# A one-layer hybrid decoder block on one core: the first 512 columns loaded slice by slice from one array, and attention issued for two pairs of heads at a time

## The chip, the core and the metric

One core of a Trainium2 chip runs one program. The metric is the device time of one execution in microseconds (us); lower is better. Engines are named as in the profile: PE (TensorE; PEld is its weight load, which runs beside its matmuls), DVE (VectorE), ACT (ScalarE), POOL (GpSimd), SP (SyncE, here only an issuer of DMAs).

## The reference, cut to what matters

256 tokens, width 1024, one layer. The normed input is multiplied with one wide matrix, whose columns feed four token mixers: a state-space scan (A), three softmax attentions (B block attention with a bias table, C with a forget-gate bias, D a sliding window with sinks; 8 heads of 64 each), and four gates.

```python
proj = h @ w_in
(m_z, m_xbc, m_dt, b_qkv, c_qkv, c_f, d_q, d_kv, gate_logits) = jnp.split(proj, SPLIT_POINTS, axis=-1)
y_a = mamba2_branch(m_z, m_xbc, m_dt, conv_w, conv_b, dt_bias, a_log, d_skip, ssm_norm_w)
y_b = moba_attention(heads(bq, N_HEADS), heads(bk, N_HEADS), heads(bv, N_HEADS), rel_bias[:, :N_HEADS])
...
# each branch is projected, scaled by its sigmoid gate and summed; w_out; residual; RMSNorm; SwiGLU; residual; RMSNorm
```

Everything is float32. A product keeps that precision by splitting each operand in two parts, "hi" (rounded) and "lo" (what is left), and adding three matmuls: hi·hi, hi·lo, lo·hi.

## The kernel before, in words

**Weights** come as a stream of pieces of about 1 MB, in the order of `FIRST` and `stream()`: `xbc0`, `xbc1`, `n0`, `qkB0`, `vB0`, ... then gates `g...`, branch projections `wb...`, `wo`, `gu` and `dn`. SP fetches a piece into one of three `raw` buffers; ACT makes its `hi` copy, DVE its `lo`. For each piece PE runs groups of matmuls: 48 matmuls of 256 columns for a piece, or 24 of 512 columns.

**The start.** `xbc0` and `xbc1` are two pieces of 256 columns. `xT` (the input, transposed) comes in six DMAs, `xbc0` in six more beside them, the channel constants `chan` in one. For each chunk ACT makes `xx` (x scaled, hi) and `hi_xbc`, DVE the lo parts, and PE follows (L440). PE has run 8 matmuls on ones before (`warm`). `xbc1` is then a piece of its own (L250 to L253), after it `n0`, whose matmuls write the tiles `n`.

**The weaver.** The order on every engine is written when the program is built. `Weaver` keeps rough clocks of PE, DVE and ACT; after each group of matmuls (`wv.tick`) it lets waiting tasks issue their next step, if their buffers are free and their DVE and ACT work ends within a slack of PE's clock. The tasks are generators; each `yield Need(...)` is a step.

**Attention** is one task for a pair of heads, `att_pair` (12 of them). Steps: a DMA of bias rows; four score matmuls into tiles `s` (L764, L766; each head uses 64 of PE's 128 rows); DVE adds the bias and takes the minimum of the negated scores (L777, L779), for C after two more operations (L849, L851); ACT takes the exponential (`p`); DVE scales `p`; PE transposes it (`pt`); ACT copies that to SBUF (`pts`); four matmuls of probabilities with values into `y` (`pv`, L685 and L687; each head uses 64 of PE's columns); ACT and DVE split `y`. The scan has one block of the same shape as `pv` for each of four pairs (`ya`). Between these blocks PE runs matmuls of the full 128 rows and columns; in the PEld rows the form stands as 128*128, 64*128 (scores) or 128*64 (`pv`). PSUM tiles of tasks come from the pool `att` (5 buffers), those of the groups from `acc` (3).

Of the kernel before, what the change touches and what calls it, by code (L numbers as in the profile page):

```python
# [199 lines left out]
def hybrid_block_kernel(ctx: ExitStack, tc: tile.TileContext, A, out):  # L200
# [225 lines left out]
    px = [att("xbc0_%d" % j, [128, 256]) for j in range(2)]  # L426
    parts["xbc0"] = h0, l0 = [wp.tile([128, WMAX], F32R, tag=n, name=n + "_xbc0", bufs=3) for n in ("hi", "lo")]
    hb, lb, wb = (cut(t, 8, 256) for t in (h0, l0, w0))
    for a, b in chunks:
        for k in range(a, b):  # L430
            act.activation(xx(k)[:, 0, :], xT[k // 4][:, k % 4, :], AF.Copy, scale=nm_mix[:, k : k + 1])
        act.activation(hb[:, a:b, :], wb[:, a:b, :], AF.Copy)
        for k in range(a, b):
            dve.scalar_tensor_tensor(xx(k)[:, 1, :], xT[k // 4][:, k % 4, :], nm_mix[:, k : k + 1],
                                     xx(k)[:, 0, :].bitcast(F32), ALU.mult, ALU.subtract)
        dve.tensor_tensor(lb[:, a:b, :], wb[:, a:b, :], hb[:, a:b, :].bitcast(F32), ALU.subtract)
        for w, i in ((hb, 0), (hb, 1), (lb, 0)):
            for k in range(a, b):
                for j in range(2):
                    pe.matmul(px[j], w[:, k, tok(j)], xx(k)[:, i, :], start=k == 0 and w is hb and i == 0,  # L440
                              stop=k == 7 and w is lb)
    wv.later(lambda: end_of("xbc0", px), [])
# [310 lines left out]
    def att_pair(br, j, heads, load_rows, q, k, vs, addend, sinks=None):  # L753
        yield Need(rows=1)
        rw = load_rows()
        yield Need()
# [13 lines left out]
        for i in range(2):  # L770
            nm_ = "%s%d" % (br, heads[i])
            s = ss[i]
            a0, a1 = addend(rw, i)
            neg = work("sp" + nm_, [128, 384], "sp")
            nm = work("nm" + nm_, [128, 2], "nm")
            init = BIG if sinks is None else sinks[:, heads[i] : heads[i] + 1]
            dve.tensor_tensor_reduce(out=neg[:, 128:384], in0=s[:, 128:384], in1=a1, scale=-1.0, scalar=init,  # L777
                                     op0=ALU.add, op1=ALU.min, accum_out=nm[:, 1:2])
            dve.tensor_tensor_reduce(out=neg[:, 0:128], in0=s[:, 0:128], in1=a0, scale=-1.0, scalar=init,  # L779
                                     op0=ALU.add, op1=ALU.min, accum_out=nm[:, 0:1])  # L780
            p = work("p" + nm_, [128, 384], "pp")
            sm = work("sm" + nm_, [128, 2], "sm")
# [11 lines left out]
        for i in range(2):  # L794
            p, sm = pp[i], sms[i]
            if sinks is not None:
                dve.tensor_tensor(sm, sm, exs[i], ALU.add)
                rel(rs=1)
# [527 lines left out]
```

## Time and profile before

| | |
|---|---|
| median of 3 runs | 521.33 us (520.48 to 521.71) |
| profiled execution, its own time | 519.55 us |
| its span, first to last instruction | 517.8 us |
| PE busy | 507.6 us, 98% of the span, 3106 matmuls |
| PE weight loads | 444.1 us |
| DVE / ACT / POOL busy | 350.6 / 284.1 / 29.7 us |
| DMA | 96.06 MB, 186 GB/s over the span |

PE is busy nearly all the time, but the matmuls are pipelined and a busy PE is not one at its peak. What can shorten the kernel is seen in the start times of PEld rows: how far apart two weight loads of the same kind stand when something lies between them.

### The profile page before, as it was taken

The numbers are of one execution on the slowest core, as the hardware profiler recorded it, in microseconds if no ns is written. First come the engines' busy times: TensorE is split into PE (matmuls) and PEld (weight loads), VectorE is DVE, ScalarE is ACT, GpSimd is POOL, SyncE is SP. The second block draws the span as 40 slices with busy tenths as digits, with TensorE's granted clock in tenths as the row PEclk, the third lists the DMA queues.
The fourth block names the chain that finished last, engine by engine and source line by source line (L and its number), as shares of the span: only waits on it lengthen the run. The fifth ranks groups of instructions, "written<-read, shape, count | busy, mean of one in ns | idle before, by whom it ended". The sixth has DMA issues, their size and how long they took to land.

```text
span 517.8 us, 7989 instructions
## 1 busy us (share of the span) xinstructions
PE 507.6 (98%) x3106; PEld 444.1 (86%) x3106; DVE 350.6 (68%) x658; ACT 284.1 (55%) x511; POOL 29.7 (6%) x61
## 2 busy tenths in 40 slices
PE   7999999999999999999999999999999999999995
PEld 6998998987897778888888899998888888888884
DVE  4577778898896947547386494688676676673435
ACT  6667464567575863443444363876655655543412
POOL 2008110012110000000000000000000000000001
PEclk8999999999999999999999999999999999999998
DMA  7974464465355244727537283355545555585302
GB/s 230 388 277 173 162 217 150 156 217 192 137 177 183 82 164 162 250 92 280 191 128 278 89 332 148 97 229 177 219 173 172 215 184 169 210 313 181 144 0 82
DMA packets 17122, 96.06 MB, mean 186 GB/s; under 512 B 2235, under 2 KB 3563, under 8 KB 6844
## 3 DMA queue, kind: packets, MB, share of 16 engines
q1 hardware_dynamic: 15660, 91.15, 48.8%
q0 software_dynamic: 1424, 4.41, 3.1%
q8 instruction: 24, 0.39, 0.3%
q14 instruction: 14, 0.11, 0.1%
HBM read 94.46 MB, written 1.09 MB: 185 GB/s over the span
## 4 chain that ended last, share of the span: by engine, by line
PE 95%; issue 2%; DMA 1%; ACT 1%; DVE 1%; SPq 0%; POOL 0%; POOLq 0%; ACTq 0%; DVEq 0%
PE pg L989 17%; PE gu L260 13%; PE pd L1186 11%; PE pb L250 8%; PE gu L262 7%; PE pvC L989 2%; PE pvB L989 2%; PE qkC L252 2%; PE po L250 1%; PE gu L250 1%; PE gu L253 1%; PE po L253 1%; PE gu L252 1%; PE qkC L250 1%; PE po L252 1%
## 5 line engine op out<-in xcount | busy, mean ns | idle before, releaser
L260 PE MATMUL gu<-x3x,hi_gu 128*128 128x512 f32 x288 | 72.1, 392 | 0.0
L989 PE MATMUL pg<-hi_g,xx 128*128 128x512 f32 x256 | 64.3, 393 | 0.0
L260 PEld LDWEIGHTS gu<-x3x,hi_gu 128*128 128x128 f32 x288 | 51.8, 189 | 9.3
L989 PEld LDWEIGHTS pg<-hi_g,xx 128*128 128x128 f32 x256 | 47.4, 188 | 11.1 <-issue 1.5
L339 DVE TENSOR_TENSOR lo_gu<-raw_gu,hi_gu 128x1024 fp32r<-128x1024 f32 x44 | 53.2, 1216 | 1.4 <-ACT hi_gu L331 1.4
L331 ACT ACTIVATE hi_g<-raw_g 128x1024 fp32r<-128x1024 f32 x32 | 32.9, 1053 | 29.0 <-DMA raw_g<-in_w_dram 14.2
L331 ACT ACTIVATE hi_gu<-raw_gu 128x1024 fp32r<-128x1024 f32 x44 | 45.6, 1051 | 1.5 <-PE gu L253 1.5
L1186 PE MATMUL pd<-hi_dn,aa 128*128 128x512 f32 (+1 forms) x176 | 46.2, 384 | 0.0
L339 DVE TENSOR_TENSOR lo_g<-raw_g,hi_g 128x1024 fp32r<-128x1024 f32 x32 | 38.1, 1219 | 8.8 <-ACT hi_g L331 8.8
L262 PEld LDWEIGHTS gu<-x3x,lo_gu 128*128 128x128 f32 x288 | 39.3, 190 | 2.8
L339 DVE TENSOR_TENSOR lo_dn<-raw_dn,hi_dn 128x1024 fp32r<-128x1024 f32 x22 | 26.1, 1220 | 21.6 <-ACT hi_dn L331 21.5
L262 PE MATMUL gu<-x3x,lo_gu 128*128 128x256 f32 x288 | 40.2, 282 | 0.0
L1186 PEld LDWEIGHTS pd<-hi_dn,aa 128*128 128x128 f32 x176 | 32.6, 188 | 6.5
L331 ACT ACTIVATE hi_dn<-raw_dn 128x1024 fp32r<-128x1024 f32 x22 | 22.4, 1052 | 25.3 <-PE pd L1186 25.3
L1128 DVE TENSOR_TENSOR gs<-gu,ge 128x256 f32<-128x256 f32 x36 | 15.3, 424 | 30.7 <-ACT ge L1127 30.6
L989 PE MATMUL pg<-lo_g,xx 128*128 128x512 f32 x128 | 34.3, 389 | 0.0
L1127 ACT ACTIVATE ge<-gu 128x256 f32<-128x256 f32 x36 | 13.5, 374 | 27.5 <-PE gu L262 27.3
L989 PEld LDWEIGHTS pg<-lo_g,xx 128*128 128x128 f32 x128 | 24.0, 188 | 5.1
L1186 PE MATMUL pd<-lo_dn,aa 128*128 128x512 f32 (+1 forms) x88 | 26.7, 384 | 0.0
L339 DVE TENSOR_TENSOR lo_wb<-raw_wb,hi_wb 128x1024 fp32r<-128x1024 f32 x16 | 19.3, 1220 | 9.3 <-ACT hi_wb L331 9.3
L913 ACT ACTIVATE gate<-pg,r1h 128x512 f32<-128x512 f32 x16 | 11.0, 687 | 25.7 <-PE pg L989 25.7
L929 DVE SCALAR_TENSOR_TENSOR gp<-gate,pb 128x512 f32<-128x512 f32 x12 | 8.2, 687 | 21.2 <-PE pb L250 20.9
(326 smaller groups left out, 1140.5 us busy)
## 6 DMA issues: line engine op xcount, KB each, us to landing
raw_gu<-in_w_dram SPq DMA_DIRECT2D x22, 1024.0 KB, 4.8
...
```

Source lines behind the costliest of these rows:

```text
L250: pe.matmul(o, l, r, start=start, stop=stop)
L252: pe.matmul(o, l, r[:, 0, :], start=start, stop=False)
L253: pe.matmul(o, l, r[:, 1, :], start=False, stop=stop)
L260: pe.matmul(o, wh(k), x(k), start=start and i == 0, stop=False)
L262: pe.matmul(o[:, 0, :], wl(k), x(k)[:, 0, :], start=False, stop=stop and i == n - 1)
L331: act.activation(parts[name][0][:, s], raws[name][:, s], AF.Copy)
L339: dve.tensor_tensor(lo[:, s], raws[name][:, s], hi[:, s].bitcast(F32), ALU.subtract)
L913: act.activation(gates[b, t][:, 512 * nh : 512 * nh + 512], p, AF.Tanh, scale=r1h[:, t : t + 1])
L989: pe.matmul(pg[t], l, r, start=kh == 0 and i == 0, stop=kh == 1 and i == len(terms) - 1)
L1127: act.activation(e[:, j, :], p[j][:, 1, :], AF.Copy)
L1128: dve.tensor_tensor(s[:, j, :], p[j][:, 0, :], e[:, j, :], ALU.add)
L1186: pe.matmul(o, l, r, start=start and j == 0, stop=stop and j == len(terms) - 1)
```

## The change

Two parts. First, `xbc0` and `xbc1` become one piece of 512 columns. Its weights are put beside `xT` in one DRAM array, `head`, after the channel constants: 64 columns of constants, and then for each of the 8 slices of the inner dimension 256 columns of `xT` and 512 of weights. SP loads it in 9 DMAs into tiles `hd0` to `hd7`; POOL's queue loads no part of it. For each slice PE runs 12 matmuls: 4 blocks of output columns, three products each. The four accumulators are two `att` and two `acc` tiles. The next pieces' DMAs (`n0`, x in natural order, `qkB0`, and now `vB0`) follow on SP.

Second, `att_quad` takes the place of `att_pair`: one task runs two pairs. The scores of both pairs are one step (8 matmuls), the transposes stay one step for each pair, and the `pv` matmuls of both pairs are one step (8 matmuls). There are 6 such tasks. A quad takes its `p`, `sm` and `pts` buffers ahead (`hold`) and needs four `att` tiles at once.

```diff
-FIRST = ("xbc0 xbc1 n0 qkB0 vB0 vB1 xbc2 qkB1 xbc3 z0 qkB2 z1 qkB3 qD0 qkC0 vC0 vC1 qkC1 qD1 qkC2 qkC3").split()
+FIRST = ("xbc0 n0 qkB0 vB0 vB1 xbc2 qkB1 xbc3 z0 qkB2 z1 qkB3 qD0 qkC0 vC0 vC1 qkC1 qD1 qkC2 qkC3").split()
...
-    cols["xbc0"], cols["xbc1"] = rng(BM0, 256), rng(CM0, 256)
+    cols["xbc0"] = rng(BM0, 512)
...
-    chunks = ((0, 1), (1, 2), (2, 4), (4, 6), (6, 7), (7, 8))
-    for a, b in chunks:
-        nc.sync.dma_start(xT[a // 4][:, a % 4 : (b - 1) % 4 + 1, :], A["xT"][:, a:b, :])
-        src = bass.AP(tensor=A["w"].tensor, offset=woff["xbc0"] + 256 * a, ap=[[2048, 128], [1, 256 * (b - a)]])
-        (nc.sync if a else pool).dma_start(w0[:, 256 * a : 256 * b], src)
-        if a == 0:
-            nc.sync.dma_start(chan, A["chan"])
-    fetch(names[1], 4)
-    fetch(names[2])
+    hd = [slot("hd%d" % i, (128, 832 if i == 0 else 768)) for i in range(8)]
+    at_ = 0
+    for i in range(8):
+        for n in (320, 512) if i == 0 else (768,):
+            o_ = 320 if n == 512 else 0
+            nc.sync.dma_start(hd[i][:, o_ : o_ + n], A["head"][:, at_ : at_ + n])
+            at_ += n
+    fetch(names[1])
...
+    px = [(att, acc)[j // 2]("xbc0_%d" % j, [128, 256]) for j in range(4)]
+    for k in range(8):
+        xk, wk_ = hd[k][:, -768:-512], hd[k][:, -512:]
+        hb, lb = (t[:, k % 4, :] for t in hl[k // 4])
+        s = hd[0][:, k : k + 1]
+        act.activation(xx(k)[:, 0, :], xk, AF.Copy, scale=s)
+        act.activation(hb, wk_, AF.Copy)
+        dve.scalar_tensor_tensor(xx(k)[:, 1, :], xk, s, xx(k)[:, 0, :].bitcast(F32), ALU.mult, ALU.subtract)
+        dve.tensor_tensor(lb, wk_, hb.bitcast(F32), ALU.subtract)
         for w, i in ((hb, 0), (hb, 1), (lb, 0)):
+            for j in range(4):
+                pe.matmul(px[j], w[:, tok(j)], xx(k)[:, i, :], start=k == 0 and w is hb and i == 0,
+                          stop=k == 7 and w is lb)
+    pool.tensor_copy(chan, hd[0][:, 0:64])
...
-    def att_pair(br, j, heads, load_rows, q, k, vs, addend, sinks=None):
+    def att_quad(br, pairs, addend, sinks=None):
...
+        yield Need(pe=1360, att=4, pp=4, sm=4)
+        hold(pp=4, sm=4)
...
+        for ss, (_, _, _, q, k, _) in zip(sss, pairs):
+            for i in range(2):
+                pe.matmul(ss[i][:, 0:128], q[hs[i], 0:128], k[hs[i], 0:128], start=True, stop=True)
+        for ss, (_, _, _, q, k, _) in zip(sss, pairs):
+            for i in range(2):
+                pe.matmul(ss[i][:, 128:384], q[hs[i], 128:256], k[hs[i], 0:256], start=True, stop=True)
...
+        yield Need(pe=1300, att=2)
+        ys = [att("y%s%d" % (br, p[0]), [128, 256]) for p in pairs]
+        for y, sts, p in zip(ys, stss, pairs):
+            pv(y, p[5], sts)
...
-    for j in range(4):
-        wv.later(lambda j=j: moba_pair(j), ["qkB%d" % j, "vB0", "vB1", "erow"], True)
+    for js in ((0, 1), (2, 3)):
+        wv.later(lambda js=js: moba_quad(js), ["qkB%d" % j for j in js] + ["vB0", "vB1", "erow"], True)
```

**SP's queue, the first rows of the program, before.** The names are tiles and DRAM arrays; sizes are partitions x float32.

```order
L395 DMA xT0_81<-in_xT_dram 128x256
L399 DMA chan_79<-in_chan_dram 128x64
L395 DMA xT0_81<-in_xT_dram 128x256
L397 DMA raw_xbc0_83<-in_w_dram 128x256
L395 DMA xT0_81<-in_xT_dram 128x512
L397 DMA raw_xbc0_83<-in_w_dram 128x512
L395 DMA xT1_82<-in_xT_dram 128x512
L397 DMA raw_xbc0_83<-in_w_dram 128x512
L395 DMA xT1_82<-in_xT_dram 128x256
L397 DMA raw_xbc0_83<-in_w_dram 128x256
L395 DMA xT1_82<-in_xT_dram 128x256
L397 DMA raw_xbc0_83<-in_w_dram 128x256
```

After these stand `xbc1` in four DMAs of 128x512 and then `n0`. The same place of the changed program:

```order
L400 DMA hd0_80<-in_head_dram 128x320
L400 DMA hd0_80<-in_head_dram 128x512
L400 DMA hd1_81<-in_head_dram 128x768
L400 DMA hd2_82<-in_head_dram 128x768
L400 DMA hd3_83<-in_head_dram 128x768
L400 DMA hd4_84<-in_head_dram 128x768
L400 DMA hd5_85<-in_head_dram 128x768
L400 DMA hd6_86<-in_head_dram 128x768
L400 DMA hd7_87<-in_head_dram 128x768
L328 DMA raw_n0_98<-in_w_dram 128x2176
L412 DMA xn0_100<-in_x_dram 128x1024
```

The bytes ahead of `n0` are the same; they are now in 9 DMAs of up to 393 KB where 17 stood (one of them POOL's), with rows of 3 KB instead of 1 or 2 KB, and each slice's `xT` and weights arrive together.

**PE after the piece `xbc3`, before**: the `y` of the first pair of B, and then the scores of its second pair (`sB2`, `sB3`), between the last matmul of `xbc3` and the first of `z0`. The scores of the first pair stand alone, 92 rows earlier.

```order
L250 MATMUL xbc3_763<-xx3_119,lo_xbc3_609 128x256 x2
L685 MATMUL yB0_850<-ptsB0_846,vB_565 64x256
L685 MATMUL yB0_850<-ptsB1_848,vB_565 64x256
L687 MATMUL yB0_850<-ptsB0_846,vB_565 64x128
L687 MATMUL yB0_850<-ptsB1_848,vB_565 64x128
L764 MATMUL sB2_858<-qkB0_438 128x128
L764 MATMUL sB3_859<-qkB0_438 128x128
L766 MATMUL sB2_858<-qkB0_438 128x256
L766 MATMUL sB3_859<-qkB0_438 128x256
L252 MATMUL z0_864<-xx0_116,hi_z0_697 128x256
```

The same place of the changed program, where the scores of both pairs stand together:

```order
L255 MATMUL xbc3_731<-xx3_117,lo_xbc3_610 128x256 x2
L774 MATMUL sB0_806<-qkB0_444 128x128
L774 MATMUL sB1_807<-qkB0_444 128x128
L774 MATMUL sB2_808<-qkB0_444 128x128
L774 MATMUL sB3_809<-qkB0_444 128x128
L777 MATMUL sB0_806<-qkB0_444 128x256
L777 MATMUL sB1_807<-qkB0_444 128x256
L777 MATMUL sB2_808<-qkB0_444 128x256
L777 MATMUL sB3_809<-qkB0_444 128x256
L257 MATMUL z0_818<-xx0_114,hi_z0_683 128x256
```

Their `y` blocks have moved to the middle of the piece `qD0`, four pieces later, also together:

```order
L255 MATMUL qD0_1179<-xx3_117,lo_qD0_1039 128x256 x2
L689 MATMUL yB0_1209<-ptsB0_1041,vB_568 64x256
L689 MATMUL yB0_1209<-ptsB1_1043,vB_568 64x256
L691 MATMUL yB0_1209<-ptsB0_1041,vB_568 64x128
L691 MATMUL yB0_1209<-ptsB1_1043,vB_568 64x128
L689 MATMUL yB1_1210<-ptsB2_1175,vB_568 64x256
L689 MATMUL yB1_1210<-ptsB3_1177,vB_568 64x256
L691 MATMUL yB1_1210<-ptsB2_1175,vB_568 64x128
L691 MATMUL yB1_1210<-ptsB3_1177,vB_568 64x128
L257 MATMUL qD0_1179<-xx0_114,hi_qD0_1038 128x256
```

Over the whole program the places where PE leaves full 128*128 matmuls for scores or `pv` go from 21 to 16. Before they are: scores alone 7 times, one `y` (or `ya`) alone 8 times, `y` and then scores 4 times, two `y` and then scores once, two `y` once. After: scores of a quad 6 times, `y` of a quad 6 times, `ya` alone 4 times. The attentions also end later: the last `y` of C stood before the first `wb` piece, and now stands in the last gate piece; D's last `y` stands before the piece that uses it, by 36 matmuls of 512 columns.

## Rows read from the trace of the kernel before

**Rows 1.** Waits of PE and of PEld: engine, line, who was waited for; us in total, times, longest.

```profile
PE xbc L440 <- ACT hi_xbc L432: 2.3, 2, 2.1
...
PE yB L685 <- ACT ptsB L815: 0.9, 1, 0.9
```

**Rows 2.** Stretches of the start: us, then busy time (instructions) of PE, PEld, DVE, ACT, POOL, the granted clock, DMA share, GB/s.

```profile
2.00:5.00 3.00, 2.86 (x14) 2.56 (x13) 0.25 (x1) 1.00 (x5) 1.74 (x5) 1.00 0.88 230
5.00:9.00 4.00, 2.08 (x12) 1.88 (x12) 1.98 (x6) 1.95 (x6) 0.00 (x0) 1.00 0.91 268
9.00:14.00 5.00, 4.74 (x27) 4.74 (x28) 4.86 (x11) 4.21 (x10) 0.00 (x0) 0.66 0.98 297
14.00:21.00 7.00, 7.00 (x61) 7.00 (x60) 3.11 (x5) 3.85 (x5) 0.00 (x0) 1.00 1.00 414
```

**Rows 3.** The start in order of time, PE, PEld and ACT: start us, us, engine, line, operation, tiles, shape, count, idle time before and who ended it.

```profile
1.08 3.78 PE L424 MATMUL warm<-cumu 128*128 128x128 f32 x16 [1.08 <-DVE cumu L383]
5.08 1.12 PE L440 MATMUL xbc<-xx,hi_xbc 128*128 128x256 f32 x4 [0.22 <-ACT hi_xbc L432]
6.28 0.64 PE L440 MATMUL xbc<-xx,hi_xbc 128*128 128x256 f32 x4
6.76 0.40 PE L440 MATMUL xbc<-xx,lo_xbc 128*128 128x256 f32 x2
9.26 2.01 PE L440 MATMUL xbc<-xx,hi_xbc 128*128 128x256 f32 x8 [2.10 <-ACT hi_xbc L432]
15.06 0.19 PEld L252 LDWEIGHTS xbc<-xx,hi_xbc 128*128 128x128 f32 x1
20.82 2.06 PEld L250 LDWEIGHTS n<-hi_n,xx 128*128 128x128 f32 x16
...
4.21 0.51 ACT L431 ACTIVATE xx<-xT,chan 128x256 fp32r<-128x256 f32 x1 [1.99 <-DMA chan<-in_chan_dram]
18.41 2.12 ACT L331 ACTIVATE hi_n<-raw_n 128x1088 fp32r<-128x1088 f32 x2 [2.15 <-DMA raw_n<-in_w_dram]
```

**Rows 4.** Groups of ACT instructions of one shape: count, busy us, mean ns of one, idle time before and who ended it.

```profile
L431 ACT ACTIVATE xx<-xT,chan 128x256 fp32r<-128x256 f32 x8 | 3.8, 500 | 4.3 <-DMA xT<-in_xT_dram 2.3 <-DMA chan<-in_chan_dram 2.0
L432 ACT ACTIVATE hi_xbc<-raw_xbc 128x512 fp32r<-128x512 f32 x2 | 1.2, 614 | 0.0
```

**Rows 5.** PEld in order of time: groups of 12 matmuls of 512 columns (`pg`, 8 hi and 4 lo) with nothing between them; here the first rows of the first and of the seventh.

```profile
268.55 1.77 PEld L989 LDWEIGHTS pg<-hi_g,xx 128*128 128x128 f32 x8
...
284.87 0.19 PEld L989 LDWEIGHTS pg<-hi_g,xx 128*128 128x128 f32 x1
```

**Rows 6.** PEld in order of time, blocks of attention between such groups.

```profile
158.79 1.68 PEld L989 LDWEIGHTS pg<-hi_g,xx 128*128 128x128 f32 x8
...
163.41 1.68 PEld L989 LDWEIGHTS pg<-hi_g,xx 128*128 128x128 f32 x8 [0.33 <-issue]
...
166.35 0.30 PEld L764 LDWEIGHTS sD<-kD,qD 64*128 64x128 f32 x4 [0.35 <-issue]
166.57 0.31 PEld L766 LDWEIGHTS sD<-kD,qD 64*128 64x128 f32 x4
167.21 0.76 PEld L989 LDWEIGHTS pg<-hi_g,xx 128*128 128x128 f32 x4 [0.33 <-issue]
...
180.57 1.68 PEld L989 LDWEIGHTS pg<-hi_g,xx 128*128 128x128 f32 x8
...
183.50 0.20 PEld L685 LDWEIGHTS yD<-ptsD,vD 128*64 128x64 f32 x4 [0.35 <-issue]
...
184.31 1.70 PEld L989 LDWEIGHTS pg<-hi_g,xx 128*128 128x128 f32 x8 [0.17 <-issue]
```

**Rows 7.** PEld in order of time: two `y` and then scores between two groups of `pvC` (12 matmuls of 512 columns), and two `y` alone between halves of `qkC` (24 matmuls of 256 columns).

```profile
112.70 1.77 PEld L989 LDWEIGHTS pvC<-hi_vC,xx 128*128 128x128 f32 x8
...
118.05 1.69 PEld L989 LDWEIGHTS pvC<-hi_vC,xx 128*128 128x128 f32 x8 [0.33 <-issue]
...
146.27 0.19 PEld L252 LDWEIGHTS qkC<-xx,hi_qkC 128*128 128x128 f32 x1
...
150.79 0.19 PEld L252 LDWEIGHTS qkC<-xx,hi_qkC 128*128 128x128 f32 x1 [0.17 <-issue]
```

**Rows 8.** Stretches, columns as in rows 2: the attention part, and the parts in which gates and branch projections run.

```profile
58.00:130.00 72.00, 71.10 (x548) 64.02 (x548) 62.61 (x147) 44.22 (x88) 7.70 (x11) 1.00 0.55 186
130.00:192.00 62.00, 62.00 (x435) 50.50 (x435) 48.89 (x160) 41.05 (x114) 3.86 (x6) 1.00 0.44 151
192.00:203.60 11.60, 11.60 (x57) 9.42 (x54) 5.80 (x7) 5.38 (x7) 0.00 (x0) 1.00 0.26 91
203.60:225.40 21.80, 21.80 (x98) 18.06 (x97) 11.27 (x10) 9.23 (x11) 0.00 (x0) 1.00 0.67 242
```

**Rows 9.** DVE groups of C's softmax, columns as in rows 4.

```profile
L851 DVE SCALAR_TENSOR_TENSOR f<-cr,cumn,amask 128x256 f32<-128x256 f32 x8 | 3.8, 477 | 0.0
L777 DVE CUSTOM_DVE_ANT_0 spC<-sC,f 128x256 f32<-128x256 f32 x8 | 3.4, 424 | 1.5 <-PE qkC L253 0.5
L849 DVE SCALAR_TENSOR_TENSOR f<-cr,cumn,amask 128x128 f32<-128x128 f32 x8 | 2.8, 345 | 0.0
L779 DVE CUSTOM_DVE_ANT_0 spC<-sC,f 128x128 f32<-128x128 f32 x8 | 2.3, 285 | 0.0
L777 DVE DVE_READ_ACCUMULATOR2_ANT nmC<- 128x1 f32 x8 | 0.7, 82 | 0.0
```

More of the change, by code (lines that the diff above doesn't have):

```diff
@@ L228, in rel, with hold @@
             wv.free[t] += n
+    def hold(**tags):
+        for t, n in tags.items():
+            wv.free[t] -= n
     def acc(name, shape=(128, 512)):
@@ L425, in hybrid_block_kernel @@
     rel(att=1)
[L426 to L436, printed above, removed]
-        for w, i in ((hb, 0), (hb, 1), (lb, 0)):
[L438 to L442, printed above, removed]
+    px = [(att, acc)[j // 2]("xbc0_%d" % j, [128, 256]) for j in range(4)]
+    hl = [[cut(wp.tile([128, WMAX], F32R, tag=n, name="%s_xbc%d" % (n, i), bufs=3), 4, 512) for n in ("hi", "lo")]
+          for i in range(2)]
+    for k in range(8):
[6 more added lines that the diff above has]
+        dve.tensor_tensor(lb, wk_, hb.bitcast(F32), ALU.subtract)
+        for w, i in ((hb, 0), (hb, 1), (lb, 0)):
+            for j in range(4):
[3 more added lines that the diff above has]
+    for i in range(2):
+        wv.later(lambda i=i: conv(i, px[2 * i : 2 * i + 2]), [])
     fetch(names[3])
@@ L770, in att_pair @@
[L770 to L782, printed above, removed]
-            act.activation(p[:, 128:384], neg[:, 128:384], AF.Exp, bias=nm[:, 1:2], scale=-1.0, accum_out=sm[:, 1:2])
-            act.activation(p[:, 0:128], neg[:, 0:128], AF.Exp, bias=nm[:, 0:1], scale=-1.0, accum_out=sm[:, 0:1])
-            if sinks is not None:
-                es = work("es" + nm_, [128, 2], "rs")
-                act.activation(es, nm, AF.Exp, bias=sink[:, heads[i] : heads[i] + 1])
-                exs.append(es)
-            pp.append(p)
-            sms.append(sm)
-            rel(att=1, sp=1, nm=1, ff=int(fox))
@@ L792, in att_pair @@
-        rel(rows=1)
-        yield Need(dve=1100, rs=2)
[L794 to L798, printed above, removed]
-            r = work("r%s%d" % (br, heads[i]), [128, 2], "rs")
-            dve.reciprocal(r, sm)
-            dve.tensor_scalar(p[:, 128:384], p[:, 128:384], r[:, 1:2], None, ALU.mult)
-            dve.tensor_scalar(p[:, 0:128], p[:, 0:128], r[:, 0:1], None, ALU.mult)
-            rel(rs=1, sm=1)
@@ new lines, in att_quad @@
+        yield Need(pe=1300, att=2)
+        ys = [att("y%s%d" % (br, p[0]), [128, 256]) for p in pairs]
+        for y, sts, p in zip(ys, stss, pairs):
+            pv(y, p[5], sts)
+            rel(pt=2)
+        for y, (j, *_) in zip(ys, pairs):
+            yield Need(act=360)
+            act.activation(yh(br, j), y, AF.Copy)
+        for y, (j, *_) in zip(ys, pairs):
+            yield Need(dve=340)
+            dve.tensor_tensor(yl(br, j), y, yh(br, j).bitcast(F32), ALU.subtract)
+            rel(att=1)
+            wv.done.add("y%s%d" % (br, j))
@@ L993, in hybrid_block_kernel @@
             continue
-        first = name in ("xbc1", "n0")
+        first = name == "n0"
         hi, lo = take(name)
@@ L1016, in hybrid_block_kernel @@
             rel(att=1)
-        if name == "xbc1":
-            wv.later(lambda p=p: end_of("xbc1", p), [])
-        elif name != "n0":
+        if name != "n0":
             wv.add(end_of(name, p))
```

160 lines of the change are left out of this document (97 added, 63 removed).

## The prediction, as it stood before the result was known

> **What bounds the kernel now.** I read the table of the page first: PE is busy in 98% of the span, so the other engines matter only where they keep PE waiting or where PE's matmuls stand further apart than they could. The waits of PE come next. They name two places after the warm-up [rows 1]: 2.3 us at the start, on ACT's `hi_xbc`, and 0.9 us once, before a `pv` block of B. That is little, so I looked at two things that a list of waits does not show.
>
> The first is the start. PE does 96 matmuls of 256 columns for `xbc0` and `xbc1`. Between 15.06 and 20.82 us it does the last 48 of them in 5.76 us, 0.12 us each [rows 3]; 96 at that pace are 11.5 us. It begins at 5.08 and is done at 20.82, so 15.74 us go into them [rows 3]: 4.2 us are lost. Two causes are in the rows. PE is idle from 7.16 (6.76 plus 0.40) to 9.26, because the third chunk of `xT` is late; and after that idle stretch 8 matmuls take 2.01 us instead of about 1, and the granted clock of 9 to 14 us is 0.66, so part of that stretch ran at the lower of the two levels, 1.2 GHz [rows 2, 3]. The first four matmuls also run at half speed (1.12 us, where four take 0.64 us from 6.28 on [rows 3]). All the while the DMAs move 230 to 297 GB/s; from 14 us on, with rows of 4 KB and more, 414 [rows 2].
>
> The second is PEld's idle time around attention. Six groups of 12 matmuls of 512 columns with nothing between them take 284.87 − 268.55 = 16.32 us, 2.72 each [rows 5]. With one block of scores behind it a group takes 167.21 − 163.41 = 3.80, so the scores cost **1.08 us**, though their own weight loads last 0.53 us (166.35 to 166.88): PEld is idle 0.35 us before them and 0.33 us behind [rows 6]. One `y` costs 184.31 − 180.57 − 2.72 = **1.02**, a `y` and then scores 163.41 − 158.79 − 2.72 = **1.90** [rows 6], two `y` and then scores 118.05 − 112.70 − 2.72 = **2.63**, and two `y` together 150.79 − 146.27 − 24 × 0.12 = **1.64** [rows 3, 7]. Together is cheaper than apart: 0.40 us for two `y`.
>
> **The change, part by part.**
>
> *Attention.* The matmuls are the same. With the blocks as counted in the section on the change, before: 7 × 1.08 + 8 × 1.02 + 4 × 1.90 + 2.63 + 1.64 = 27.6 us. After: six `y` pairs at 1.64 (9.8), four `ya` at 1.02 (4.1), and six score blocks of two pairs, a form that no row shows. Its bounds: 2 × 1.08 = 2.16 if nothing is shared; 1.08 + 0.44 = 1.52 if the second pair adds only twice the 0.22 us by which L766 follows L764 [rows 6]. I take 1.08 + 0.53 = 1.61, the second pair adding the length of its own weight loads, because the measured two `y` behave like that: the second adds 0.62 there. So after is 9.7 + 9.8 + 4.1 = 23.6, a gain of **4.0 us** (0.7 with 2.16; 4.5 with 1.52).
>
> What the row shows for the switch is 0.33 to 0.35 us idle between full and half-array weight loads, and 0.17 us behind a `y` [rows 6]. The Trainium skill (TensorEngine Tiling (Array Packing), Key Properties) says that changing the tiling mode, "not just tile", drains TensorE. By that rule the second pair's scores, in the same mode as the first's, pay no drain, and the sum stays; if each block of scores paid one whatever stands before it, six score blocks would cost 2.16 and the sum would lose 3.3 us. The trace agrees for `y`; for scores no run has shown it yet.
>
> DVE and ACT do the same instructions as before, later. I cost that at nothing. What hides it: DVE is 79% busy at 130 to 192 us, where C and D ran, and about half busy at 192 to 225, where much of them goes [rows 8]. If the cover is gone, see rival 3. The one wait of 0.9 us before a `y` of B [rows 1] may vanish or come back at another place; I count 0.
>
> *The start.* Before the first matmul: `chan` and the first `xT`, 160 KB, let ACT begin at 4.21 [rows 3]; the first DMA of `head` has the same 160 KB, so ACT begins there again. The first weights are now 256 KB behind it on the same queue, at 230 to 268 GB/s [rows 2] another 1.1 us: 5.3. With 0.61 for hi [rows 4] PE starts at 5.9, **0.8 later** than now. From then on ACT needs 0.50 + 0.61 = 1.11 us a slice [rows 4], PE 12 × 0.12 = 1.44, the DMAs 393 KB at 297 GB/s [rows 2] 1.32. PE is the slowest, so it does not idle, and its clock has no reason to fall as it did at 9 us. It would be done at 5.9 + 8 × 1.44 = 17.4; with one slice at half speed at first, as the first four matmuls are now, at 18.8.
>
> Then `n0`. Its weights are behind the same bytes as before, about 4.3 MB, and land at 18.41 now [rows 3], half hidden by PE's late end of `xbc1`. At the same landing, PE could begin `n0` at 18.41 + 1.11 (half of hi, from 2.12 for both [rows 3]) + 0.25 = 19.8 instead of 20.82: a gain of 1.0 at least. With rows of 3 KB I expect a rate between 297 and 414 [rows 2]. An estimate from those two: the 3.2 MB of `head` end about 1.1 us earlier at 320 than at the 285 of now, the piece of `n0` follows at full rate as now, and a little less of x comes between: landing near 17.0, `n0` on PE at 18.4. Gain **2.4 us**; the ends are 1.0 (landing unchanged) and 3.4 (PE's own 17.4). What follows: x for the norm and `qkB0` lie behind in the same order and at the same rate, and ACT's squares and hi are done before PE has run `n0` (6 us), so the shift is kept. The accumulators of 512 columns take two `acc` tiles, which DVE frees before `pvB0` needs them, by a few tenths; a wait there is inside the ends.
>
> *Sum.* 519.55 (the profiled execution: 517.8 span and 1.75 around it) − 4.0 − 2.4 = 513.15. The median shown is 521.33, 1.78 above that execution; since a median is forecast, I subtract from it: **514.9 us**.
>
> **Rivals.**
>
> 1. *Scores share nothing.* Each pair's scores pay their own way even side by side. For it: scores and `y` idle differently (0.33 behind scores, 0.17 behind `y` [rows 6]). Against: two `y` do share [rows 7]. Gain 0.7 + 2.4 = 3.1: **518.2**.
> 2. *The start stays with the DMAs.* Fewer and larger rows bring no more bytes a second, `n0` lands at 18.41 as now. For it: the rate was already with rows of 1 to 2 KB near 300 at a DMA share of 0.91 to 0.98 [rows 2], that is, with engines full. Against: 414 from 14 us on [rows 2]. Gain 4.0 + 1.0: **516.3**.
> 3. *DVE's backlog stops PE* (the other side). The place: the two quads of C, which now lie between branch projections and gates. A quad brings DVE 4 × (0.477 + 0.345 + 0.424 + 0.285 + 2 × 0.082) = 6.8 us of bias and reduction [rows 9]. In the stretch of `pb` of 11.6 us DVE has 5.8 us free, half of it behind the scores [rows 8], so 3.9 us are left over; if lo parts of the next weights queue behind them, PE waits 3.9 us a quad, 7.8 for both: 521.33 − 6.4 + 7.8 = **522.7**. It decides from 6.4 us of waits on, four fifths of that backlog. For it: DVE executes in order, and C's softmax is its heaviest. Against: the same work ran in 130 to 192 us at 79% with no wait of PE [rows 1, 8], weights are split up to two pieces ahead, and the gates that follow leave DVE half free.
>
> **How the numbers follow.** Chances: my forecast 0.62 (511.8 to 517.5 by itself), rival 1 0.11, rival 2 0.11, rival 3 0.16. Rival 3 can take any part of its price: 0.07 of it I put within 0.2% of now and 0.09 above. 0.2% (1.04 us) is about what a measurement of this kernel can tell from no change. Faster: 0.62 + 0.11 + 0.11 = 0.84; the same 0.07; slower 0.09. The range reaches from 511.3 (attention 4.5, start 3.4, the one wait gone and a little for the runs' spread of 0.6) to 519.6, above rivals 1 and 2, below rival 3.
>
> **What the changed profile would show.** If right: no idle of PE between the first slice and `n0`, a granted clock of 1.00 from about 9 us on, the first weight load of `n` near 18.4; blocks of four heads' scores that cost about 1.6 us between groups and pairs of `y` at 1.6; the waits of PE as short as now. Rival 1: the second pair's weight loads start 0.3 us or more behind the first's end. Rival 2: `hi_n` waits for its DMA until 18.4. Rival 3: waits of PE or PEld on a `lo` or on `hi` in the stretches of `pb` and `pg`. I would be wrong altogether if a quad, holding four of five `att` tiles, kept a small task back that a later piece needs, or if a bad clock level stayed through the start because of the longer gap ahead of the first slice (4.86 to 5.9).

## The result, and the profile after

| | before | changed |
|---|---|---|
| median | 521.29 us (520.48 to 521.71) | 515.61 us (514.95 to 516.49) |
| ratio | | 0.9894 (95%: 0.9874 to 0.9914) |
| profiled execution, its span | 519.55, 517.8 us | 515.27, 513.5 us |
| first weight load of `n` | 20.82 us [rows 3] | 18.70 us |

The median is 5.7 us lower. Part of that is the spread of the runs: the two profiled executions, on which all readings below rest, differ by 4.3 us, and 23 later runs of the kernel before have a median of 520.58 us.

The start in order of time, selected rows (start us, us, engine, line, operation, tiles, shape, count, idle before and who ended it):

```profile
2.99 0.51 ACT L436 ACTIVATE xx<-hd 128x256 fp32r<-128x256 f32 x1 [0.77 <-DMA hd<-in_head_dram]
4.70 1.51 PE L442 MATMUL xbc<-xx,hi_xbc 128*128 128x256 f32 x8
6.45 0.51 ACT L436 ACTIVATE xx<-hd,hd 128x256 fp32r<-128x256 f32 x1 [1.80 <-DMA hd<-in_head_dram]
7.53 1.22 PE L442 MATMUL xbc<-xx,hi_xbc 128*128 128x256 f32 x8 [0.84 <-ACT hi_xbc L437]
9.83 1.21 PE L442 MATMUL xbc<-xx,hi_xbc 128*128 128x256 f32 x8 [0.60 <-ACT hi_xbc L437]
...
17.00 2.12 ACT L336 ACTIVATE hi_n<-raw_n 128x1088 fp32r<-128x1088 f32 x2 [1.64 <-DMA raw_n<-in_w_dram]
18.34 0.64 PE L442 MATMUL xbc<-xx,lo_xbc 128*128 128x256 f32 x4
18.70 2.06 PEld L255 LDWEIGHTS n<-hi_n,xx 128*128 128x128 f32 x16
```

Its stretches, which answer to [rows 2] (us, then busy time of PE, PEld, DVE, ACT, POOL, granted clock, DMA share, GB/s):

```profile
2.00:5.00 3.00, 3.00 (x15) 2.86 (x14) 0.80 (x2) 1.34 (x4) 1.33 (x3) 1.00 0.97 299
5.00:9.00 4.00, 3.16 (x24) 2.96 (x23) 1.55 (x3) 1.28 (x3) 0.00 (x0) 1.00 0.88 211
9.00:14.00 5.00, 4.40 (x34) 3.99 (x34) 4.15 (x8) 4.33 (x10) 0.00 (x0) 1.00 1.03 419
14.00:21.00 7.00, 7.00 (x60) 7.00 (x59) 4.68 (x7) 5.36 (x8) 0.00 (x0) 1.00 1.02 416
```

PE begins 0.4 us earlier than before, not later: ACT has the first `xT` and the constants at 2.99 us instead of 4.21 [rows 3]. PE waits 0.84 and 0.60 us for slices 1 and 2, because at 5 to 9 us the DMAs move only 211 GB/s. From 9 us on they move 419, from 13 us on PE runs a slice in 1.44 us, and the clock stays at 1.00, where before it was 0.66 at 9 to 14 us. The matmuls of `n` do not wait for their weights: half of `hi_n` is ready by about 18.1 us (half way through the 2.12 us from 17.00), while PE is still at its last slice. The waits of PE after the warm-up, which answer to [rows 1]:

```profile
PE xbc L442 <- ACT hi_xbc L437: 1.4, 2, 0.8
...
PE cum_n L255 <- POOL av L555: 0.9, 1, 0.9
```

The wait ahead of `yB` is gone; one on POOL's `av` is new. (Seen from the weight loads, PEld, the three waits for slices are 2.1 us and the one on `av` 1.1.) PEld in order of time, one head's columns in the form of the whole array (`cb`), then a block of two pairs' scores and one of two `y`, which answer to [rows 6, 7]:

```profile
56.95 0.30 PEld L665 LDWEIGHTS cb<-bc,bc 128*128 128x128 f32 x2
...
57.60 0.19 PEld L257 LDWEIGHTS xbc<-xx,hi_xbc 128*128 128x128 f32 x1
...
111.78 1.77 PEld L1016 LDWEIGHTS pvC<-hi_vC,xx 128*128 128x128 f32 x8
...
114.28 0.19 PEld L1016 LDWEIGHTS pvC<-lo_vC,xx 128*128 128x128 f32 x1
...
114.82 0.52 PEld L774 LDWEIGHTS sB<-qkB 64*128 64x128 f32 x8 [0.35 <-issue]
115.26 0.74 PEld L777 LDWEIGHTS sB<-qkB 64*128 64x128 f32 x8
116.33 0.76 PEld L1016 LDWEIGHTS pvC<-hi_vC,xx 128*128 128x128 f32 x4 [0.33 <-issue]
...
165.90 1.67 PEld L1016 LDWEIGHTS pg<-hi_g,xx 128*128 128x128 f32 x8
...
170.28 0.77 PEld L1016 LDWEIGHTS pg<-hi_g,xx 128*128 128x128 f32 x4 [0.17 <-issue]
```

The score block costs 116.33 − 111.78 − 2.72 = 1.83 us; the six cost 1.71 to 1.83, 1.79 in the mean. Two `y` cost 170.28 − 165.90 − 2.72 = 1.66. One head's 384 columns of f32 take the whole array 0.65 us (`cb`, 57.60 − 56.95).

These costs differ by up to 0.1 us with what stands ahead of the group of 12 matmuls. A measure without that goes from the start of the last weight load ahead of a block to the first behind it. In the kernel before, for one pair's scores, it begins at

```profile
165.81 0.19 PEld L989 LDWEIGHTS pg<-lo_g,xx 128*128 128x128 f32 x1
```

and ends at 167.21 [rows 6]: 1.40 us. For two pairs it is 116.33 − 114.28 = 2.05 us. In the same way one `y` takes 1.34 us before and two `y` 1.99 after, both between groups of `pg`. A second pair adds 0.65 us in both kinds of block.

**Where the 4.8 us came from.** The table has the first weight load of three stages in each run, from the groups of these tiles. `pvB` comes ahead of all attention, `mt` behind all of it; from `mt` to the end all runs take 220.0 to 220.9 us, but for head_b01_late (221.7). Each row is one profiled execution; the runs that stand below the first two rows are told in the next section.

| run | `n` | `pvB` | `mt` | `pvB` to `mt` | median |
|---|---|---|---|---|---|
| before | 20.8 | 32.8 | 297.8 | 265.0 | 521.29 |
| changed | 18.7 | 30.7 | 293.0 | 262.3 | 515.61 |
| head_only | 19.3 | 31.3 | 300.2 | 268.9 | 521.48 |
| quads_only | 21.4 | 33.4 | 294.4 | 261.0 | 516.65 |
| head_b0_late | 18.5 | 30.5 | 299.5 | 269.0 | 521.77 |
| head_b01_late | 19.1 | 31.1 | 296.6 | 265.5 | 519.04 |
| before_b0_late | 21.4 | 33.4 | 301.0 | 267.6 | 522.74 |
| full_ahead | 18.7 | 30.7 | 294.3 | 263.6 | 516.32 |
| full_between | 17.9 | 29.9 | 297.6 | 267.7 | 520.47 |
| scores_128 | 21.5 | 33.5 | 296.6 | 263.1 | 516.42 |
| cum_later | 18.4 | 30.4 | 291.5 | 261.0 | 514.44 |
| rows_later | 17.7 | 29.7 | 291.9 | 262.3 | 514.32 |
| rows_cum | 17.9 | 29.9 | 291.0 | 261.0 | 514.39 |
| rows_cum_ssd | 17.1 | 29.1 | 289.5 | 260.3 | 512.33 |

Of the changed kernel's 4.8 us at `mt`, 2.1 come from the start and 2.7 from the stretch of attention; behind `mt` it loses 0.5 again. The start varies from one execution to the next: with the old one `n` stands at 20.8 to 21.4 us in three runs, with the new one of the changed kernel at 17.9 to 19.3 in seven, and at 21.5 in scores_128. There PE waited 2.9 us for one slice, and the granted clock of 9 to 14 us was 0.88. So the 2.1 us are those of one execution.

### The profile page after: what moved, and what is told of

It is laid out like the page before. It is cut to its first block, busy times and chain, and to the rows that moved or that the text cites. A ratio compares the mean times of both kernels' runs of the same rounds, so it can differ in the third digit from the quotient of the medians.

```text
span 513.5 us, 7958 instructions
## 1 busy us (share of the span) xinstructions
PE 503.6 (98%) x3106; PEld 441.9 (86%) x3106; DVE 350.2 (68%) x657; ACT 284.4 (55%) x509; POOL 31.5 (6%) x61
## 4 chain that ended last, share of the span: by engine, by line
PE 92%; POOL 3%; DVE 2%; issue 1%; DMA 1%; ACT 0%; SPq 0%; POOLq 0%; ACTq 0%
PE pg L1016 17%; PE gu L265 13%; PE pd L1211 11%; PE pb L255 9%; PE gu L267 7%; PE pvC L1016 2%; PE xbc L442 2%; PE qkC L257 2%; PE po L255 1%; PE gu L255 1%; PE po L258 1%; PE qkC L255 1%; PE gu L258 1%; PE gu L257 1%; PE qkC L258 1%; PE po L257 1%
## 5 line engine op out<-in xcount | busy, mean ns | idle before, releaser
L336 ACT ACTIVATE hi_g<-raw_g 128x1024 fp32r<-128x1024 f32 x32 | 32.7, 1051 | 17.9 <-DMA raw_g<-in_w_dram 8.3
L344 DVE TENSOR_TENSOR lo_dn<-raw_dn,hi_dn 128x1024 fp32r<-128x1024 f32 x22 | 26.1, 1220 | 21.6 <-ACT hi_dn L336 21.5
L1153 DVE TENSOR_TENSOR gs<-gu,ge 128x256 f32<-128x256 f32 x36 | 15.3, 424 | 30.7 <-ACT ge L1152 30.6
L336 ACT ACTIVATE hi_wb<-raw_wb 128x1024 fp32r<-128x1024 f32 x16 | 16.7, 1055 | 6.8 <-PE pg L1016 6.8
```

What stands on the lines that cost most here:

```text
L336: act.activation(parts[name][0][:, s], raws[name][:, s], AF.Copy)
L344: dve.tensor_tensor(lo[:, s], raws[name][:, s], hi[:, s].bitcast(F32), ALU.subtract)
L1153: dve.tensor_tensor(s[:, j, :], p[j][:, 0, :], e[:, j, :], ALU.add)
```

## The experiments

**Each part alone.** One run takes the new `head` with the old `att_pair`, the other the old start with `att_quad`.

```diff
-    def att_quad(br, pairs, addend, sinks=None):
+    def att_pair(br, j, heads, load_rows, q, k, vs, addend, sinks=None):
...
```

> The changed kernel with the attention of before (pairs of heads one by one); only the first piece is new. Theory: the two halves of the change add up, and the 2.12 us by which the first matmul of `n0` comes earlier in the changed kernel (18.82 against 20.94) are kept to the end. The blocks of attention fall a little differently from before (9 scores alone, 7 `y` alone, 2 `ya` alone, three joint `y` and scores, two joint `y`: 9 x 1.08 + 9 x 1.02 + 3 x 1.90 + 2 x 1.64 = 27.9 us against 27.6), so 521.3 - 2.1 + 0.3 = 519.5 us, ratio 0.9965; `n0` on PE near 18.8, `mt` about 1.8 us earlier than before. Rival: the start's gain is lost at a later wait (the one of PE on `av`, 0.9 us in the changed kernel, is its first sign): 520.4 or more, ratio above 0.998.

```diff
-    hd = [slot("hd%d" % i, (128, 832 if i == 0 else 768)) for i in range(8)]
+    xT = [slot("xT%d" % i) for i in range(2)]
...
```

> The kernel before with attention on two pairs of heads at a time; its start is untouched. Theory: six score blocks at 1.79, six pairs of `y` at 1.65 and four `ya` at 1.02 are 24.7 us against 27.6 before, and the wait of 0.9 us before a `y` of B goes: 521.3 - 2.9 - 0.5 (half of the wait, since one of 0.5 us on `lo_g` came up in the changed kernel) = 517.9 us, ratio 0.9935. Rival A, the prediction's own size: 4.0 us from the blocks, 517.3, ratio 0.992. Rival B, the scores share nothing: score blocks of 2.16, 520.6, ratio 0.9987.

Measured: the first piece alone 521.48 us, ratio 1.0013 (0.9998 to 1.0027); the quads alone 516.65, 0.993 (0.9908 to 0.9952). The parts do not add: 0.7 us more and 3.6 us less make 3.0 less, both together 5.5. The first piece alone brings `n` 1.5 us earlier and loses 3.9 us between `pvB` and `mt`. Its waits of PE, the stretch, and DVE in order of time:

```profile
PE cum_t L567 <- DVE rB L806: 1.5, 1, 1.5
...
PE yB L689 <- ACT ptsB L821: 0.9, 1, 0.9
```

```profile
55.00:60.00 5.00, 3.35 (x26) 2.66 (x24) 3.61 (x17) 3.21 (x11) 0.00 (x0) 1.00 0.23 60
60.00:65.00 5.00, 4.89 (x27) 4.70 (x27) 5.00 (x10) 4.00 (x9) 1.07 (x2) 0.66 0.50 200
```

```profile
49.97 1.21 DVE L344 TENSOR_TENSOR lo_xbc<-raw_xbc,hi_xbc 128x1024 fp32r<-128x1024 f32 x1
56.32 0.42 DVE L783 CUSTOM_DVE_ANT_0 spB<-sB,bB 128x256 f32<-128x256 f32 x1 [5.14 <-DMA bB<-erow]
```

DVE stands 5.1 us before the bias rows of B's first pair, and what is behind it (`cumn`, `rB`, lo parts) makes PE idle for 1.65 us at 55 to 60; then the mean granted clock of 60 to 65 us is 0.66, so PE is at 1.2 GHz for part of it. The two make up the loss: PEld's waits between `pvB` and `mt` on `cum_t`, `ptB` and `yB` are 3.7 us where the kernel before has 1.5, and 5 us at a mean of 0.66 are by estimate 1.7 us of full speed, 3.9 together. The DMA of `bB` is on POOL's queue, behind the chain for `av`. POOL in order of time, before and changed:

```profile
38.45 0.76 POOL L530 TENSOR_SCALAR sp_d<-sp_e 128x32 f32<-128x32 f32 x1 [14.76 <-ACT ea L528]
39.68 1.10 POOL L535 TENSOR_TENSOR sp_s<-sp_e,sp_d 128x32 f32<-128x32 f32 x1 [0.47 <-DVE sp_d L532]
...
51.39 0.20 POOL L551 COPY av<-dt 128x16 f32<-128x16 f32 x1
```

```profile
35.42 0.44 POOL L534 TENSOR_SCALAR sp_d<-sp_e 128x32 f32<-128x32 f32 x1 [13.21 <-ACT ea L532]
38.97 1.10 POOL L539 TENSOR_TENSOR sp_s<-sp_e,sp_d 128x32 f32<-128x32 f32 x1 [3.11 <-DVE sp_d L536]
...
52.29 0.20 POOL L555 COPY av<-dt 128x16 f32<-128x16 f32 x1
```

The new start lets POOL begin 3.0 us earlier, but it then waits 3.1 us for DVE's reciprocal, and from `sp_s` on the chain takes 13.5 us instead of 11.9 (why is open). So it ends 0.9 us later than before, not 2 us earlier. PE, 2 us ahead, meets it: in the changed kernel at `cum_n`, with the first piece alone by way of `bB` and DVE.

**B's first pair later.** Three runs ask whether that wait is the cause.

```diff
-        wv.later(lambda j=j: moba_pair(j), ["qkB%d" % j, "vB0", "vB1", "erow"], True)
+        wv.later(lambda j=j: moba_pair(j), ["qkB%d" % max(j, 1), "vB0", "vB1", "erow"], True)
```

> The new first piece with the attention of before (as in the run with the first piece alone), but the first pair of B may not begin ahead of the piece `qkB1`, so that its scores stand some 12 us later, near where the first block of two pairs stands in the changed kernel. Theory: the run with the first piece alone lost the start's gain because DVE stood 5.1 us before the first pair's bias rows `bB`, which queue on POOL behind its chain for `av` (done at 52 us whatever the start); with the scores later DVE does not wait there, and about 4 us come back: 517.4 us, ratio 0.9925 (516.7 to 518.2). Rival: what is missing there is DVE's time as a whole (the convolutions and the softmax of B in 45 to 80 us); then the wait comes back at another instruction and the time stays above 520.

Measured: 521.77 us, 1.0008 (0.9989 to 1.0028). This theory fell, and the rival held: DVE no longer waits for `bB`, a wait comes back at another instruction, and the time stays. The waits of PE, and ACT in order of time:

```profile
PE yB L689 <- ACT ptsB L821: 2.2, 1, 2.2
PE cum_n L255 <- POOL av L555: 1.1, 1, 1.1
```

```profile
78.52 0.63 ACT L642 ACTIVATE cu<-cc 128x512 f32<-128x512 f32 x1 [4.70 <-DVE cc L640]
...
80.00 0.85 ACT L821 ACTIVATE ptsB<-ptB 128x384 f32<-128x384 f32 x2
```

On ACT `ptsB` stands behind a convolution step for which ACT waits 4.7 us on DVE, and PE waits for `ptsB`. Here too the granted clock falls behind PE's wait (columns as in [rows 2]):

```profile
80.00:85.00 5.00, 4.48 (x23) 3.76 (x24) 4.33 (x9) 4.05 (x10) 0.39 (x1) 0.66 0.59 210
```

PEld's waits are 2.4 us more than in the kernel before, the low clock costs 1.7 by the same estimate, and the stretch is 4.0 us longer.

The same line with `max(j, 2)` holds both first pairs back further:

> The new first piece with the attention of before, and no pair of B may begin ahead of the piece `qkB2`, about 24 us later than in the run with the first piece alone. With the first pair held back to `qkB1`, DVE no longer waited for the bias rows, but PE then waited 2.2 us for `ptsB`, which stood on ACT behind a convolution step that DVE brought late. Theory: it is the place of B's first `y` that counts, in a stretch (72 to 82 us) in which DVE is busy all the time; the blocks of two pairs put it later, and with it later here too the start's gain comes back: blocks 27.7 us as before, the waits ahead of `yB` gone (1.6), the new one of 1.1 on `av` left, n0 at 18.7: 518.0 us (517.3 to 518.8), ratio 0.994. Rival: DVE is late as a whole between 60 and 100 us, wherever the pair stands; a wait of the same size comes up at another instruction, 520.5 or more.

Measured: 519.04 us, 0.9974 (0.9956 to 0.9992). `pvB` to `mt` takes 265.5 us instead of 268.9, with no wait of PE in it but 0.9 us on `av`, and the clock stays at 1.00. Most of the loss is back; 1 us less came than expected. PE leaves full matmuls for scores or `pv` at 23 places here instead of 21, which by the start times costs 1.0 us more. The line with `max(j, 1)` in the kernel before:

> The kernel before with this one thing changed: the first pair of B may not begin ahead of `qkB1`. It measures how much of the quads' own gain is the later place of the first scores and not the blocks. Theory: the two waits ahead of `yB` (1.3 and 0.3 us of PEld in the kernel before) go and the blocks come to 27.8 us instead of 27.6: 521.1 - 1.4 = 519.7, ratio 0.9973; then about 2.5 us of the 3.7 us that the quads alone brought belong to the blocks. Rival: the wait returns at `ptsB`, as in the run with the new first piece: 521 to 522.

Measured: 522.74 us, 1.0032 (1.0012 to 1.0053), the rival. Its wait, and the stretch behind it:

```profile
PE yB L685 <- ACT ptsB L815: 2.2, 1, 2.2
```

```profile
82.00:87.00 5.00, 5.00 (x28) 4.19 (x29) 4.14 (x8) 3.84 (x8) 0.55 (x1) 0.66 0.57 210
```

So the wait at B's first `y` hangs on where that `y` stands against DVE's convolutions, with the old start as with the new, and the low clock behind it costs another 1.7 us by the estimate. `att_quad` issues it only when both pairs are ready, and no run with quads waits there.

**What a pair shares.** A matmul of the whole array between the two pairs of a block, and the same one ahead of the block, for scores (shown) and for `y`:

```diff
+            if n_ == 1:        # the control: n_ == 0
+                pe.matmul(sss[1][0][:, 0:128], xx(0)[:, 0, 0:128], xx(0)[:, 0, 0:128], start=True, stop=True)
...
```

> The changed kernel with one more matmul of the full array (128x128 with 128 columns, its result overwritten at once) between the two pairs in each of the six score blocks and the six blocks of two `y`; scores are issued pair by pair. Theory: what the pairs share is the change between full and half array, about 0.4 us a block (1.08 for one pair's scores, 0.67 to 0.71 for the second pair; 1.02 and 0.64 for `y`). The matmul in the middle takes that sharing away: score blocks go from 1.79 to about 2.25, `y` blocks from 1.65 to 2.1, 12 x 0.4 = 4.8 us more than with the same matmul ahead of the block, 520.5 to 521.2 us in all. Rival 1 of the prediction (scores share nothing): score blocks as with the matmul ahead, only the `y` blocks longer, 518.5 to 519.

> The control to the run with the matmul between the pairs: the same added matmul of the full array, ahead of the first pair of each block, where the array is full anyway. Theory: 12 x 0.06 to 0.1 us, score blocks of about 1.85, `y` blocks of about 1.7, 516.3 to 516.8 us. Rival: the order pair by pair or an added matmul costs more than its columns; then blocks of 2 us and more here too, and the difference to the other run says little on the switch.

Measured: 520.47 us with it between, 516.32 with it ahead. PEld in order of time, the same block, first with the matmul between and then ahead:

```profile
111.99 1.77 PEld L1019 LDWEIGHTS pvC<-hi_vC,xx 128*128 128x128 f32 x8
...
115.24 0.31 PEld L778 LDWEIGHTS sB<-qkB 64*128 64x128 f32 x4
115.88 0.19 PEld L774 LDWEIGHTS sB<-xx 128*128 128x128 f32 x1 [0.33 <-issue]
...
116.99 1.69 PEld L1019 LDWEIGHTS pvC<-hi_vC,xx 128*128 128x128 f32 x8 [0.33 <-issue]
```

```profile
112.45 1.77 PEld L1019 LDWEIGHTS pvC<-hi_vC,xx 128*128 128x128 f32 x8
...
115.77 0.31 PEld L778 LDWEIGHTS sB<-qkB 64*128 64x128 f32 x4
116.09 0.41 PEld L776 LDWEIGHTS sB<-qkB 64*128 64x128 f32 x4
...
117.06 1.69 PEld L1019 LDWEIGHTS pvC<-hi_vC,xx 128*128 128x128 f32 x8 [0.33 <-issue]
```

Blocks: 116.99 − 111.99 − 2.72 = 2.28 us against 117.06 − 112.45 − 2.72 = 1.89; in the mean of the six, 2.25 against 1.85, and for `y` 2.06 against 1.72. That is 12 × 0.37 = 4.4 us by the rows and 4.1 by the stretch and the medians. The second pair's loads follow the first's without a gap (116.09) where nothing is between, and behind 0.33 us idle and the added matmul where something is. Rival 1 is out.

**What the second pair costs.**

```diff
-                pe.matmul(ss[i][:, 128:384], q[hs[i], 128:256], k[hs[i], 0:256], start=True, stop=True)
+                for c in range(2):
+                    pe.matmul(ss[i][:, tok(1 + c)], q[hs[i], 128:256], k[hs[i], tok(c)], start=True, stop=True)
```

> The changed kernel with each score matmul of 256 columns made as two of 128: the same columns, six matmuls a pair instead of four. Theory: a second pair costs its columns (384 columns of f32, which one matmul form of the whole array, `cb`, takes 0.65 us for), so nothing changes: score blocks of 1.75 to 1.85, 515.6 us. Rival, the prediction's step: a second pair costs the length of its weight loads (0.53 us for four); with six it is 0.8, so 0.54 us more a block, 2.3 us each, 3.2 us in all: 518.8.

Measured: 516.42 us, 0.9907 (0.9886 to 0.9928), and in order of time:

```profile
114.69 1.77 PEld L1017 LDWEIGHTS pvC<-hi_vC,xx 128*128 128x128 f32 x8
...
118.17 1.08 PEld L778 LDWEIGHTS sB<-qkB 64*128 64x128 f32 x16
119.37 1.68 PEld L1017 LDWEIGHTS pvC<-hi_vC,xx 128*128 128x128 f32 x8
```

119.37 − 114.69 − 2.72 = 1.96 us, 0.13 more than in the changed kernel, and 0.9 us more from `pvB` to `mt`. Half as many loads again for the same columns cost 0.13 a block where the rival wanted 0.54, so the length of the loads is not the price. That the columns are rests on the equal 0.65 us of a second pair and of `cb`; no run changes the columns. The idle time of PEld behind the block is 0.12 us here (118.17 + 1.08 to 119.37) and 0.33 in the changed kernel, so it is no fixed price of the change of form.

**The wait on `av`.**

```diff
-        yield Need(pool=7000)
+        yield Need(pool=9500)
```

> The changed kernel, with the planner told that POOL's chain behind `n0` takes 9.5 us instead of 7.0, so that the matmuls of `cum_n` stand one half of `qkB` later. Theory: PE's wait of 0.9 us on POOL's `av` goes and nothing takes its place: 515.6 - 0.9 = 514.7, ratio 0.9877. Rival: what hangs on `cum_n` (the decay rows of the state space part and of C) is then late itself, and a wait of about the same length comes up before the first `ya`: 515.6, ratio 0.9894.

Measured: 514.44 us, 0.9884 (0.9864 to 0.9904). The wait is gone, `pvB` to `mt` takes 261.0 us, 1.25 less, about as much as PEld's wait there (1.1). The intervals of this ratio and the changed kernel's overlap; the stretch shows the gain, the median alone would not.

**The dip at 5 to 9 us.**

```diff
-    pool.dma_start(rows, bass.AP(tensor=A["rows"].tensor, offset=0, ap=[[0, 128], [1, 32]]))
...
         nc.sync.dma_start(xn[t], A["x"][tok(t), :])
+    nc.sync.dma_start(rows, bass.AP(tensor=A["rows"].tensor, offset=0, ap=[[0, 128], [1, 32]]))
```

> The changed kernel, with the DMA of `rows` (16 KB, one 128-byte row to all 128 partitions) taken from POOL's queue, where it was issued at 2.5 us, and put on SP's queue behind the two DMAs of `xn`. Theory: it is this transfer that takes the DMA engines' time at 6.5 to 8.5 us, where they are busy for a share of 0.84 to 1.06 and move only 146 to 216 GB/s; without it the slices 1 and 2 land earlier, PE's waits of 0.84 and 0.60 us on `hi_xbc` shrink to 0.4 or less in sum, `n0` is on PE at 17.4 to 18.0 instead of 18.82, and the time is 0.8 to 1.4 us under the changed kernel's: 514.2 to 514.8, ratio 0.987. Rival: the dip belongs to the slices themselves (3 KB rows, first transfers of a queue); rate and waits stay, 515.6, ratio 0.9894.

Measured: 514.32 us, 0.9884 (0.9865 to 0.9903). DMA queues at 5 to 9 us, POOL's queue alone (packets, MB, share of the 16 engines' time), in the kernel before, the changed one and this one:

```profile
q0 software_dynamic: 64, 0.02, 2.3%
```

```profile
q0 software_dynamic: 61, 0.02, 23.8%
```

```profile
q0 software_dynamic: 32, 0.00, 0.6%
```

and its stretch and its piece `n0`:

```profile
5.00:9.00 4.00, 3.36 (x23) 3.15 (x23) 2.10 (x5) 2.46 (x6) 0.00 (x0) 1.00 1.01 341
```

```profile
15.00 2.11 ACT L336 ACTIVATE hi_n<-raw_n 128x1088 fp32r<-128x1088 f32 x2 [1.62 <-DMA raw_n<-in_w_dram]
```

Without `rows` there the DMAs move 341 GB/s instead of 211, the weights of `n0` land 2.0 us earlier, and `n` is on PE at 17.79 instead of 18.82; one wait of 0.6 us for a slice is left. One execution would say little on `n`, and this ratio's interval overlaps the changed kernel's too, but the rate does not: at 5 to 9 us it is 341 to 365 GB/s in the three runs with this change and 198 to 277 in the eight that have the new start without it. ACT begins `hi_n` at 14.9 to 15.7 us in the three and at 16.2 to 17.8 in the eight. The rival is out.

**Together.** Both repairs:

> The changed kernel with both repairs: `rows` on SP's queue behind `xn`, and `cum_n` one half of `qkB` later. Theory: they are at different places and add up (each alone brought 1.2 to 1.3 us against the changed kernel): 515.6 - 2.4 = 513.2 us, ratio 0.984 to 0.985. Rival: with the start another 1.0 us earlier POOL's chain for `av` is the end that PE meets again, and half of it comes back as a wait: 514.3.

Measured: 514.39 us, 0.9878 (0.9852 to 0.9904; 513.17 to 515.0). Inconclusive: `pvB` to `mt` has the whole gain of the later `cum_n` (261.0) and the profiled execution took 513.17, but the median is no lower than that of either repair alone. It is the rival's number, without its wait: PE waits for no `av` in this run.

And with the four `ya` in two blocks:

```diff
-    for j in range(4):
-        wv.later(lambda j=j: ssd_pair(j), ["xc%d" % j, "cb%d" % (j // 2), "cum", "z%d" % (j // 2)], True)
+    for i in range(2):
+        wv.later(lambda i=i: ssd_quad((2 * i, 2 * i + 1)), ["xc%d" % (2 * i), "xc%d" % (2 * i + 1), "cb%d" % i, "cum", "z%d" % i], True)
```

`ssd_quad` has the steps of `ssd_pair` for two pairs, and issues the `pv` of both in one step, as `att_quad` does.

> The same two repairs, and the four `ya` of the state space part in two blocks of two pairs, as the attention's `y` are. Theory: two blocks of 1.65 in place of four of 1.02, 0.8 us less: 512.4 us, ratio 0.983. Rival: the second pair's decay comes late for the joint block (DVE is busy nearly all the time at 70 to 85 us), and PE waits at it for more than the 0.8: 513.2 or more.

Measured: 512.33 us, 0.9843 (0.9816 to 0.987), the fastest, 2.7 us under the changed kernel by the ratios, with the whole interval below the changed kernel's. The stretch is 0.7 us shorter than with the repairs alone, and the waits of PE after the warm-up have nothing behind the start:

```profile
PE xbc L442 <- ACT hi_xbc L437: 0.5, 2, 0.3
```

## Why the prediction was right, step by step

- **Time.** 514.9 was forecast, 515.61 measured, inside the range. The two gains were each a little too large, and what was counted as nothing did come to nearly nothing. That it is off by only 0.7 us is in part luck: between the profiled executions the gain is 4.3 us, where 6.4 were forecast.
- **Attention blocks: 4.0 us forecast, 2.9 by the rows.** Two `y` at 1.66 and `ya` at 1.01 were as taken, scores 1.79 instead of 1.61: 6 × 1.79 + 6 × 1.65 + 4 × 1.01 = 24.7 against 27.6. The step that was mis-sized is "the second pair adding the length of its own weight loads", 0.53. It adds 0.71 in the mean by the same kind of sum, and 0.65 from load to load. That fits a pair's columns: `cb` takes 0.65 us for the columns of one head, and a pair's two heads side by side as long. `scores_128` shows that the loads have little to do with it. The two `y`, where the second adds 0.62 (0.65 from load to load), had looked like loads and fit columns as well.
- **The switch.** What a pair saves is the change of form, 0.34 to 0.40 us. The Trainium skill's rule (TensorEngine Tiling (Array Packing), Key Properties), that a change of the tiling mode drains TensorE and not the next tile in the same mode, agrees with the two runs with an added matmul: the loads stand idle only where the form changes.
- **"0" for the wait of 0.9 us.** Right by luck, because two things offset each other. The waits ahead of `yB` went (1.5 us in PEld's waits before); 1.1 us on `av` and 0.5 on a `lo_g` behind the second quad of C came. 2.9 + 1.5 − 1.6 is 2.8, and the stretch shows 2.7. The `lo_g` is all there was of rival 3.
- **Start: 2.4 us forecast, 2.1 measured.** "0.8 later" for the first matmul was wrong: 4.70 us. The step that failed there is "so ACT begins there again": the one DMA that brings constants and `xT` together let ACT begin at 2.99 us, not at 4.21, and at 2.97 to 3.09 in all ten other runs with the new start. The 4.21 was itself late; the two other runs with the old start have 3.40. The weights came 1.03 us behind that, near the 1.1 of the forecast. "PE does not idle" was wrong: 1.4 us of waits, 2.1 by PEld. The two errors nearly cancelled. The landing near 17.0 was right, but unlike in the forecast `n` did not hang on it: PE's own slices ended later. The clock at 1.00 was right here, and is not safe: see scores_128.
- **"The shift is kept"** held in the changed kernel and is the weakest step. I followed it to `qkB0` and stopped. The new first piece alone keeps nothing: PE meets B's first pair, which POOL's chain, DVE and ACT bring no earlier, and behind that wait the clock falls. With the quads that pair's `y` stands later, and 2.5 us of the 5.5 exist only with both parts. For the first part alone the forecast would have failed: 2.4 us less expected, 0.7 more measured. Which of DVE's instructions would have to move for the pairs to keep the start's gain is open: holding the first pair back to `qkB1` did not do it, holding both back to `qkB2` gave back most of it.
- **Rival 2** was half true: the rate was low where it expected, for another reason, the transfer of `rows`.
